# Narrow Fourier matmuls merged or left out, folded weights made in 64-column halves, rows of a coming pair loaded ahead of weight stores

## The chip, the cores and the metric
The kernel runs on one core of a Trainium2 chip. The metric is the device time of one execution in microseconds (us); several executions are timed and the median counts. One further execution was recorded by the profiler. A core has five engines that run side by side, each through its own instructions in order: TensorE (PE; its weight loads are listed as PEld), VectorE (DVE), ScalarE (ACT), GpSimd (POOL) and SyncE (SP), which here does nothing but issue transfers.

## The reference
Two sequences of 1024 tokens by 1024 features go through one encoder layer. Cut to what matters:

```python
mod = silu(c) @ w_ada + b_ada                      # shift, scale, gate, twice
h = rmsnorm(x, g_mix) * (1 + sc1) + sh1
z = h @ w_in                                       # q_lat 256 | kv_lat 128 | k_pe 64 | f_in 512
y_mla = mla_group(q_lat, kv_lat, k_pe, ...)        # 4 heads of attention from the latents
fr = real(fft2(f_in as (1024, 8 groups, 64), axes=(1, 3), norm='ortho'))
y_four = einsum('bsgc,gcd->bsgd', fr, w_four)      # 64 x 64 per group
x = x + ga1 * (concat([y_mla, y_four]) @ w_out)
h2 = rmsnorm(x, g_ffn) * (1 + sc2) + sh2
x = x + ga2 * ((silu(h2 @ w_gate) * (h2 @ w_up)) @ w_down)
return rmsnorm(x, g_final)
```

## The kernel before
All is float32. A large product is made exact enough by splitting both operands into a rounded high part and a remainder (`split`: a cast by ScalarE, a subtraction by VectorE, lines 60 and 61) and by three matmuls (`mm3`, lines 71 to 73). So most rows of TensorE read L71, L72 or L73, and the tile names tell them apart. Small products (L207, L303, L306, L744) are plain float32, and each of those leaves two records in the trace.

**Stage 1**, up to about 245 us. The tokens are taken in eight `pairs` (s, j): sequence s, and the rows of block j in both halves of the sequence (u = 0, 1). For a pair, `norm` loads its two row blocks `xt` (SP) and scales them (VectorE), `flip` transposes and modulates them, `zproj` makes the latents (`lat`, from the pool tag `sk` of three buffers), `latents` transposes and stores those, `evenodd` makes the sum and the difference of the two halves (`eoh`, `eol`), and `fourier_in` multiplies these by the input weights with the first cosine or sine transform folded in (`wcs_h`, `wcs_l`). Sums go to `zc`, differences to `zs`. For j = 0 another product gives the cosine columns of the difference's first row: `zo`, made of two token columns (24 matmuls, `128*2 128x280`). The cosine part holds 256 columns and 24 more, the Nyquist column of each of the eight groups three times over, for high part, high part and remainder.

`pair(k)` writes out this order, with the pieces of the generator `extras` between: at each `next(more)` it goes on to its next `yield`. Its last part folds the Fourier weights: `w4` (made into `lw`) times the last four chunks of `w_out` (`wo4`), times the gate `ga` of each sequence, stored to `wm_d` and `wn_d` (Nyquist rows). The products `so` take buffers of `sk` too.

**Stage 2**, about 245 to 349 us. `zsplit` splits `zc`, `zs` and `zo`, `dft` multiplies by the tables of the transform along the tokens (`tb`) into `A` (cosine), `B` (sine) and `ny` (Nyquist), `prep_wm` loads and splits the folded weights into `wm` and `wn`, and `fourier_out` makes, for a block j and a column half g, `pa` from A, wm and the 24-row product of `ny` and `wn` (L702), `pb` from B, and their difference and sum `ed`, which go to `fo_d`. For j = 0 the row of frequency 0 is put right: `dc_prep` makes `dl`, a product with it and two with columns of `ny` (L714, L715) go to three banks `pn`, and VectorE adds them to one row of `ed`. `mod2` (L744) makes the second modulation between. All accumulators come from eight banks.

**Stage 3**, from 349 us, is attention by blocks of 256 queries, and from about 1000 us to the end the FFN runs. Neither is changed. The loads for attention stand on SP between stores of `fo_d`.

Of the kernel before, what the change touches and what calls it, by code (L numbers as in the profile page):

```python
# [12 lines left out]
F32 = mybir.dt.float32  # L13
# [8 lines left out]
P = 128  # L22
# [22 lines left out]
NCS = NZC + NZS  # L45
NTE = 258
# [4 lines left out]
def hybrid_encoder_kernel(ctx: ExitStack, tc: tile.TileContext, a: dict):  # L51
# [33 lines left out]
    cmask = const.tile([P, 4], F32, name="cmask")  # L85
# [28 lines left out]
    wn_d = [dram.tile([NNYQ, D], F32, name=f"wn_d{s}") for s in range(2)]  # L114
# [39 lines left out]
    zo = [zp.tile([2, NZC], F32, name=f"zo{s}") for s in range(2)]  # L154

    with ExitStack() as st:
# [23 lines left out]
        lw = w.tile([P, 4, 2 * 64 + NNYQ], F32, name="lw")  # L180
# [72 lines left out]
        def small_weights():  # L253
            w4 = w.tile([P, 4, 2, GD], F32, tag="gah0", name="w4")
            nc.sync.dma_start(w4, a["w4"])
            for b in range(2):
                pr = slice(64 * b, 64 * b + 64)
                for k, op in enumerate((ALU.add, ALU.subtract)):
                    nc.vector.tensor_tensor(out=lw[pr, :, 64 * k + 32 * b : 64 * k + 32 * b + 32], in0=w4[pr, :, 0, 0:32],
                                            in1=w4[pr, :, 1, 0:32], op=op)  # L260
                for p in range(4):
                    o = P + 2 * p + b
                    nc.vector.tensor_copy(lw[pr, p, o : o + 17 : 8],
                                          w4[pr, p, 0, 32:33].broadcast_to([64, 3]))

        def extras():
# [27 lines left out]
            for g in range(2):  # L294
                gs = slice(512 * g, 512 * g + 512)
                ga = [w.tile([P, 512], F32, tag=f"gah{s}", name="gah") for s in range(2)]
                for s in range(2):
                    nc.sync.dma_start(ga[s], ga_d[32 * g + s, :].partition_broadcast(P))
                yield
                for p in range(5):  # L300
                    ps = bank()
                    if p < 4:
                        nc.tensor.matmul(ps, lw[:, p, :P], wo4[p // 2][:, p % 2, gs], start=True, stop=True)  # L303
                    else:
                        for q in range(4):
                            nc.tensor.matmul(ps[:NNYQ, :], lw[:, q, P:], wo4[q // 2][:, q % 2, gs], start=(q == 0), stop=(q == 3))  # L306
                    n = P if p < 4 else NNYQ
                    for s in range(2):
                        so = stile("so")
                        nc.vector.tensor_tensor(out=so[:n], in0=ps[:n], in1=ga[s][:n], op=ALU.mult)  # L310
                        if p < 4:
                            for k in range(2):
                                nc.sync.dma_start(wm_d[s][64 * (p % 2) : 64 * (p % 2) + 64, 2 * k + p // 2, gs],
                                                  so[64 * k : 64 * k + 64, :])
                        else:
                            nc.sync.dma_start(wn_d[s][:, gs], so[:n])
                    if p % 2 == 1:
                        yield
# [28 lines left out]

        def norm(k):
            s, j = pairs[k]
            ms = tiny.tile([P, 2], F32, name="ms")  # L350
            xt = []
            for u in range(2):
                t = xtile()
                nc.sync.dma_start(t, xs[s][rows(j, u), :])
                jk = w.tile([P, D], BF16, tag="junk", name="junk", bufs=1)
                nc.scalar.activation(jk, t, AF.Square, scale=1.0 / 32.0, accum_out=ms[:, u : u + 1])
                xt.append(t)
            r = rstd(ms, 2)
            for u in range(2):
                nc.vector.tensor_scalar(out=xt[u], in0=xt[u], scalar1=r[:, u : u + 1], scalar2=None, op0=ALU.mult)  # L360
            st1["x", k] = xt
# [76 lines left out]
        def fourier_in(k, i):  # L438
# [68 lines left out]
        def pair(k):  # L507
# [90 lines left out]
    with ExitStack() as st:  # L598
# [8 lines left out]
        zh, wms = {}, {}  # L607

        def zsplit(s):
            z = [[wa.tile([P, 4, n], F32R, tag=f"z{k}{i}", name=f"zh{k}{i}", bufs=1) for i in range(2)]  # L610
                 for k, n in enumerate((NZC, NZS))]
            od = [wa.tile([P, NZC], F32R, tag=f"zo{i}", name=f"zod{i}", bufs=1) for i in range(2)]
            for k, src in enumerate((zc[s], zs[s])):
                for c in range(0, 4, 2):
                    split(z[k][0][:, c : c + 2], z[k][1][:, c : c + 2], src[:, c : c + 2])
            for i in range(2):
                nc.vector.tensor_copy(od[i], rd(z[0][i][:, 0, :]))
            split(od[0][0:1, :], od[1][0:1, :], zo[s][0:1, :])
            zh[s] = (z, od)

        def dft(s):
# [3 lines left out]
            ny = w.tile([NNYQ, NT], F32R, tag="ny", name="ny", bufs=1)  # L625
            for q in (0, 2, 1):
                m = NNYQ if q == 2 else P
                sl = slice(P * q, P * q + m)
                pe, po = bank2(), bank2()
                for c in range(4):  # L630
                    mm3(pe[:m, :NTE], z[0][0][:, c, sl], z[0][1][:, c, sl], tb[0][0][:, c, :NTE], tb[0][1][:, c, :NTE],
                        c == 0, c == 3)
                for c in range(4):
                    zz = [od[i][:, sl] if c == 0 else z[0][i][:, c, sl] for i in range(2)]
                    mm3(po[:m, :256], zz[0], zz[1], tb[0][0][:, c, NTE:NT], tb[0][1][:, c, NTE:NT], c == 0, c == 3)
                if q == 2:
                    ah = w.tile([NNYQ, NT], F32R, tag="nyh", name="nyh", bufs=1)
                    al = w.tile([NNYQ, NT], F32, tag="nyl", name="nyl", bufs=1)
# [4 lines left out]
                if q == 2:  # L643
                    nc.vector.tensor_scalar(out=al, in0=al, scalar1=cmask[:m, 1:2], scalar2=None, op0=ALU.mult)
                    nc.vector.scalar_tensor_tensor(out=ny, in0=rd(ah), scalar=cmask[:m, 0:1], in1=al,
# [7 lines left out]
            return A, B, ny  # L653

        def prep_wm(s):
            wm = [w.tile([P, 4, D], F32R, tag=f"wm{i}", name=f"wm{i}", bufs=1) for i in range(2)]
            wn = w.tile([NNYQ, D], F32R, tag="wn", name="wn", bufs=1)
            for c in range(4):
                for g in range(2):
# [3 lines left out]
                    split(wm[0][:, c, gs], wm[1][:, c, gs], raw)  # L663
            for g in range(2):
                gs = slice(512 * g, 512 * g + 512)
                wnr = w.tile([NNYQ, 512], F32, tag="wnr", name="wnr", bufs=1)
                wnh = w.tile([NNYQ, 512], F32R, tag="wnh", name="wnh", bufs=1)
                nc.sync.dma_start(wnr, wn_d[s][:, gs])
                nc.scalar.copy(wnh, wnr)
                nc.vector.tensor_tensor(out=wnr, in0=wnr, in1=rd(wnh), op=ALU.subtract)  # L670
                nc.vector.tensor_scalar(out=wnr, in0=wnr, scalar1=cmask[:NNYQ, 3:4], scalar2=None, op0=ALU.mult)
                nc.vector.scalar_tensor_tensor(out=wn[:, gs], in0=rd(wnh), scalar=cmask[:NNYQ, 2:3], in1=wnr,
                                               op0=ALU.mult, op1=ALU.add)
            wms[s] = (wm, wn)

        def dc_prep(s, ABn):
            A = ABn[0]
            dl = [w.tile([P, 2, 2], F32R, tag=f"dl{i}", name=f"dl{i}", bufs=1) for i in range(2)]
            cd = w.tile([P, 2], F32, tag="cd", name="cd", bufs=1)
            ce = w.tile([P, 2], F32, tag="ce", name="ce", bufs=1)  # L680
            sub(cd, rd(A[0][:, :, 512]), rd(A[0][:, :, 0]), nc.vector)
            sub(ce, rd(A[1][:, :, 512]), rd(A[1][:, :, 0]), nc.vector)
            add(cd, cd, ce, nc.vector)
            for e in range(2):
                nc.vector.tensor_copy(dl[0][:, :, e], cd)
                nc.vector.tensor_tensor(out=dl[1][:, :, e], in0=cd, in1=rd(dl[0][:, :, e]), op=ALU.subtract)
            dls[s] = dl

        dls = {}

        def fourier_out(s, ABn, j):
# [3 lines left out]
            if j == 0:  # L695
                dl = dls.pop(s)
            for g in range(2):
# [23 lines left out]
        zsplit(0)  # L721
        tb[1] = [wa.tile([P, 4, 512], F32R, name=f"tb1{i}") for i in range(2)]
# [30 lines left out]
        for s in range(2):  # L753
            for j in (1, 2, 3, 0):
                fourier_out(s, abn, j)
                if j == 1:
                    dc_prep(s, abn)
# [751 lines left out]
def _constants():  # L1509
# [24 lines left out]
    cmask = np.zeros((P, 4))  # L1534
# [4 lines left out]
    cmask[8:16, 3] = 1  # L1539
    r = {  # L1540
# [55 lines left out]
```

## Time and profile before

| | us |
|---|---|
| median of 3 runs | 2136.97 (2136.36 to 2138.33) |
| the profiled execution | 2136.0 |
| its span | 2134.2 |
| mean granted clock of TensorE | 0.989 |

The profile covers the span; the 1.8 us between span and time lie around it, and the profiled execution is 0.97 us under the median. In a row of the timeline stand the start, the duration, engine, line, operation, out<-in, for a matmul the weights (rows by columns) and the streamed operand, the number of instructions that the row sums, and in brackets the engine's idle time before and what ended it. Matmuls overlap: the time that one costs is the distance from its start to the next start. In a row of the windows stand the window, its length, busy time and instructions of TensorE, of its weight loads, of VectorE, ScalarE and GpSimd, the granted clock, the DMA engines' busy share and GB/s.

### The profile page before, as it was taken

To read this page: it belongs to the slowest core of one execution; us is meant where nothing else is said; L and a number is where in the kernel's file an instruction comes from. 1 tells how busy PE (TensorE), PEld (TensorE's weight loads), DVE (VectorE), ACT (ScalarE), POOL (GpSimd) and SP (SyncE) were. 2 spreads that over 40 slices of the span, in tenths; PEclk is the share of its full clock that TensorE was granted. 3 is DMA by queue.
4 is the path that set the end of the run, shared out by engine and by line. 5 is a ranking of instruction groups with operands and counts; after the bars stand their busy time and mean duration, and the time that the engine had idled before them with its cause. 6 is when DMAs were issued, how large, how long until landed. Compare 5 with 4: busy or idle time off the path is not lost. (4 is left out here: it accounts for less than half of the span.)

```text
span 2134.2 us, 28930 instructions
## 1 busy us (share of the span) xinstructions
PE 2054.9 (96%) x10096; PEld 1671.4 (78%) x10096; DVE 1420.7 (67%) x2118; ACT 904.3 (42%) x1758; POOL 826.7 (39%) x1014
## 2 busy tenths in 40 slices
PE   5899998999999998999999999999999999999998
PEld 3787865888888886888888888887788888888876
DVE  2656655766676668786677667777866566557675
ACT  2655522555564546333333336444333333336441
POOL 1455202111222313797797720135545445420142
PEclk8999999999999999999999999999999999999999
DMA  9586656433545355564455468675423222248662
GB/s 366 189 248 181 225 189 234 102 92 92 138 119 124 119 182 203 187 212 168 159 206 188 153 227 290 226 237 175 148 79 119 99 101 97 99 135 290 230 226 101
DMA packets 184387, 371.11 MB, mean 174 GB/s; under 512 B 19280, under 2 KB 58832, under 8 KB 181168
## 3 DMA queue, kind: packets, MB, share of 16 engines
q1 hardware_dynamic: 166384, 313.80, 44.3%
q0 software_dynamic: 17856, 55.45, 8.8%
q8 instruction: 79, 1.29, 0.2%
q14 instruction: 68, 0.56, 0.1%
HBM read 257.18 MB, written 120.39 MB: 177 GB/s over the span
## 5 line engine op out<-in xcount | busy, mean ns | idle before, releaser
L71 PE MATMUL bank<-H,wh 128*128 128x512 f32 x1232 | 489.4, 397 | 13.5 <-DVE val L130 5.0
L73 PE MATMUL bank<-H,wl 128*128 128x512 f32 x1232 | 488.1, 396 | 1.5 <-DVE wl L61 1.5
L72 PE MATMUL bank<-H,wh 128*128 128x512 f32 x1232 | 488.2, 396 | 0.0
L130 DVE TENSOR_TENSOR val<-bank,val 128x512 f32<-128x512 f32 x244 | 167.0, 689 | 191.2 <-PE bank L73 183.4
L71 PEld LDWEIGHTS bank<-H,wh 128*128 128x128 f32 x1232 | 232.2, 188 | 73.2 <-DVE val L130 7.3
L73 PEld LDWEIGHTS bank<-H,wl 128*128 128x128 f32 x1232 | 232.0, 188 | 58.5 <-DVE wl L61 2.3
L72 PEld LDWEIGHTS bank<-H,wh 128*128 128x128 f32 x1232 | 232.0, 188 | 55.8
L61 DVE TENSOR_TENSOR wl<-draw,wh 128x512 fp32r<-128x512 f32 x286 | 200.9, 737 | 80.9 <-ACT wh L60 79.8
L60 ACT CAST wh<-draw 128x512 fp32r<-128x512 f32 x286 | 169.3, 619 | 155.3 <-PE bank L72 76.9
L72 PE MATMUL bank<-wl,wh 128*128 128x512 f32 x572 | 223.7, 391 | 2.2 <-DVE wl L61 2.2
L130 POOL TENSOR_TENSOR val<-val 128x512 f32<-128x512 f32 x58 | 82.8, 1434 | 363.5 <-DVE val L1380 188.6
L73 PE MATMUL bank<-wh,wl 128*128 128x512 f32 x572 | 222.6, 389 | 0.0
L71 PE MATMUL bank<-wh 128*128 128x512 f32 x572 | 222.6, 389 | 0.0
L60 ACT CAST wh<-rgu 128x512 fp32r<-128x512 f32 x172 | 106.7, 621 | 269.4 <-PE bank L72 211.5
L60 ACT CAST wh<-val 128x512 fp32r<-128x512 f32 x133 | 82.2, 621 | 277.6 <-PE bank L72 249.4
L61 DVE TENSOR_TENSOR wl<-val,wh 128x512 fp32r<-128x512 f32 x133 | 139.3, 1049 | 83.5 <-ACT wh L60 83.5
L61 DVE TENSOR_TENSOR wl<-rgu,wh 128x512 fp32r<-128x512 f32 x172 | 167.1, 972 | 4.8 <-ACT wh L60 4.2
L127 POOL TENSOR_TENSOR val<-rgu 128x512 f32<-128x512 f32 x84 | 122.0, 1452 | 120.3 <-DMA rgu<-in_wgu_dram 92.5
L72 PEld LDWEIGHTS bank<-wl,wh 128*128 128x128 f32 x572 | 107.3, 188 | 27.7 <-DVE wl L61 5.7
L71 PEld LDWEIGHTS bank<-wh 128*128 128x128 f32 x572 | 107.4, 188 | 22.3
L73 PEld LDWEIGHTS bank<-wh,wl 128*128 128x128 f32 x572 | 107.4, 188 | 22.1
L127 POOL TENSOR_TENSOR val<-val 128x512 f32<-128x512 f32 x89 | 119.4, 1358 | 1.3
(319 smaller groups left out, 4096.7 us busy)
## 6 DMA issues: line engine op xcount, KB each, us to landing
rgu<-in_wgu_dram SPq DMA_DIRECT2D x86, 512.0 KB, 4.2
draw<-s_d SPq DMA_DIRECT2D x143, 256.0 KB, 4.1
s_d<-val POOLq DMA_DIRECT2D x88, 256.0 KB, 4.1
draw<-t_d SPq DMA_DIRECT2D x88, 256.0 KB, 4.3
s_d<-val SPq DMA_DIRECT2D x66, 256.0 KB, 2.7
draw<-in_w_down_dram SPq DMA_DIRECT2D x55, 256.0 KB, 4.0
wada<-in_w_ada_dram SPq DMA_DIRECT2D x13, 1024.0 KB, 8.8
xt<-in_x_dram SPq DMA_DIRECT2D x16, 512.0 KB, 6.3
```

Source lines behind the costliest of these rows:

```text
L60: here["a"] = nc.scalar.copy(hi, src).ins
L61: here["v"] = nc.vector.tensor_tensor(out=lo, in0=src, in1=rd(hi), op=ALU.subtract).ins
L71: nc.tensor.matmul(out, lh, rh, start=first, stop=False, skip_group_check=cont)
L72: nc.tensor.matmul(out, lh, rl, start=False, stop=False, skip_group_check=cont)
L73: nc.tensor.matmul(out, ll, rh, start=False, stop=last, skip_group_check=cont)
L127: eng.tensor_tensor(out=out, in0=x, in1=y, op=ALU.subtract)
L130: eng.tensor_tensor(out=out, in0=x, in1=y, op=ALU.add)
```

## The change
1. `zo` of both sequences is made at once, at pair (1, 0): four token columns `zoc`, two of each sequence, which VectorE copies aside; the row of sequence 1 is moved to a tile of its own by a transfer.
2. The fold is made by chunk c of `wm`: the two 64-column halves of `lw` that make a chunk go to partitions 0 to 63 and 64 to 127 of one bank, one store of 128 rows takes the place of two of 64, and the Nyquist rows are no product of their own: they are rows 0, 32, 64 and 96 of the sine chunks, stored three times over by a transfer (`wn_d`), and put to zero in `wm` by a column of `cmask`, when `wm` is split.
3. The Nyquist columns of both sequences are split together (`nyq_split`) and go through `dft` once, 48 columns wide, at sequence 0. `ny` and `wn` are padded with zero rows to 128; `cmask` picks the sequence's rows.
4. `dc_prep` goes. The DC row is made by columns 512 and 513 of A and `ny` in one bank, and ScalarE copies it over the row of `ed`.
5. `x_load(k + 2)`, the loads of `norm(k + 2)`, stands before the third `next(more)` of pair k, and no longer after it.

```diff
-    zo = [zp.tile([2, NZC], F32, name=f"zo{s}") for s in range(2)]
+    zo = [zp.tile([ZOW, NZC], F32, name="zo"), zp.tile([1, NZC], F32, name="zo1")]
...
-                for p in range(5):
+                for c in range(4):
+                    k, i = c // 2, c % 2
                     ps = bank()
-                    if p < 4:
-                        nc.tensor.matmul(ps, lw[:, p, :P], wo4[p // 2][:, p % 2, gs], start=True, stop=True)
-                    else:
-                        for q in range(4):
-                            nc.tensor.matmul(ps[:NNYQ, :], lw[:, q, P:], wo4[q // 2][:, q % 2, gs], start=(q == 0), stop=(q == 3))
+                    for q in range(2):
+                        nc.tensor.matmul(ps[64 * q : 64 * q + 64, :], lw[:, 2 * i + q, 64 * k : 64 * k + 64], wo4[i][:, q, gs],
+                                         start=True, stop=True)
                     for s in range(2):
                         so = stile("so")
...
+                        nc.vector.tensor_tensor(out=so, in0=ps, in1=ga[s], op=ALU.mult)
+                        nc.sync.dma_start(wm_d[s][:, c, gs], so)
+                        if k == 1:
+                            nc.sync.dma_start(
+                                wn_d[NNYQ * s : NNYQ * s + NNYQ, gs].rearrange("(k r) n -> r k n", k=3)[4 * i : 4 * i + 4],
+                                so[0:97:32, :].unsqueeze(1).broadcast_to([4, 3, 512]))
...
             if i == 1 and j == 0:
+                for k in range(2):
+                    nc.vector.tensor_copy(zoc[k][:, :, 2 * s : 2 * s + 2], rd(eo[1][k][:, :, 0:2]))
+            if i == 1 and j == 0 and s == 1:
                 po = bank()
                 for c in range(NC):
-                    mm3(po[:2, :NZC], eo[1][0][:, c, 0:2], eo[1][1][:, c, 0:2], wcs_h[:, c, :NZC], wcs_l[:, c, :NZC],
+                    mm3(po[:ZOW, :NZC], zoc[0][:, c, :], zoc[1][:, c, :], wcs_h[:, c, :NZC], wcs_l[:, c, :NZC],
                         c == 0, c == NC - 1)
-                nc.vector.tensor_copy(zo[s], po[:2, :NZC])
+                nc.vector.tensor_copy(zo[0], po[:ZOW, :NZC])
+                nc.sync.dma_start(zo[1], zo[0][2:3, :])
...
+            if k + 2 < nk:
+                x_load(k + 2)
             next(more, None)
...
+        nyt = w.tile([P, NT], F32R, name="ny")
+        nc.vector.tensor_scalar(out=nyt, in0=raws[0, 0], scalar1=0.0, scalar2=None, op0=ALU.mult)
...
-            for q in (0, 2, 1):
-                m = NNYQ if q == 2 else P
+            for q in (0, 2, 1) if s == 0 else (0, 1):
+                m = NY2 if q == 2 else P
...
-                wnr = w.tile([NNYQ, 512], F32, tag="wnr", name="wnr", bufs=1)
-                wnh = w.tile([NNYQ, 512], F32R, tag="wnh", name="wnh", bufs=1)
-                nc.sync.dma_start(wnr, wn_d[s][:, gs])
+                wnr = w.tile([P, 512], F32, tag="wnr", name="wnr", bufs=1)
+                wnh = w.tile([P, 512], F32R, tag="wnh", name="wnh", bufs=1)
+                nc.gpsimd.memset(wnr, 0.0)
+                nc.sync.dma_start(wnr[:NY2], wn_d[:, gs])
...
                 if j == 0:
-                    pn = [bank2() for _ in range(3)]
+                    pn = bank2()
                     for q in range(2):
-                        mm3(pn[0][:2, :], dl[0][:, q, :], dl[1][:, q, :], wm[0][:, q, gs], wm[1][:, q, gs], q == 0, q == 1)
-                    nc.tensor.matmul(pn[1][:2, :], ny[:, 512:514], wn[:, gs], start=True, stop=True)
-                    nc.tensor.matmul(pn[2][:2, :], ny[:, 0:2], wn[:, gs], start=True, stop=True)
-                    for q, f in enumerate((add, add, sub)):
-                        f(ed[1][0:1, :], ed[1][0:1, :], pn[q][0:1, :], nc.vector)
+                        mm3(pn[:2, :], A[0][:, q, 512:514], A[1][:, q, 512:514], wm[0][:, q, gs], wm[1][:, q, gs], q == 0, False)
+                    nc.tensor.matmul(pn[:2, :], ny[:, 512:514], wn[:, gs], start=False, stop=True)
+                    nc.scalar.copy(ed[1][0:1, :], pn[0:1, :])
```

Where the instructions stand, in the rows' own words (the line, the operation, out<-in, the shape of the output and the count; lines 71 to 73 before are 73 to 75 after). TensorE at the first fold burst, before, where `ident,xt` is a flip and `wcs_h,eoh` is `fourier_in`:

```order
L431 MATMUL bank<-ident,lat 128x128 x4
L374 MATMUL bank<-ident,xt 128x128 x8
L303 MATMUL bank<-wada,lw 128x512 x2
L71 MATMUL bank<-wcs_h,eoh 128x280
L72 MATMUL bank<-wcs_l,eoh 128x280
```
and at the first of the two 24-column bursts, where `wz_h,hh` is `zproj`:

```order
L73 MATMUL bank<-wz_h,hl 128x448
L374 MATMUL bank<-ident,xt 128x128 x8
L306 MATMUL bank<-wada,lw 24x512 x4
L71 MATMUL bank<-wz_h,hh 128x448
L72 MATMUL bank<-wz_l,hh 128x448
```
After, at the first fold burst:

```order
L432 MATMUL bank<-ident,lat 128x128 x4
L375 MATMUL bank<-ident,xt 128x128 x8
L304 MATMUL bank<-wada,lw 64x512 x4
L73 MATMUL bank<-wcs_h,eoh 128x280
L74 MATMUL bank<-wcs_l,eoh 128x280
```
Four products of 64 columns stand where two of 128 stood, and no burst stands between the flip and `zproj` any more.

TensorE at the end of a unit for j = 0, from the last product of B on, before:

```order
L73 MATMUL bank<-wm_3394,B_3262 128x512
L71 MATMUL bank<-wm_3394,dl_3544 2x512
L72 MATMUL bank<-wm_3395,dl_3544 2x512
L73 MATMUL bank<-wm_3394,dl_3545 2x512
L71 MATMUL bank<-wm_3394,dl_3544 2x512
L72 MATMUL bank<-wm_3395,dl_3544 2x512
L73 MATMUL bank<-wm_3394,dl_3545 2x512
L714 MATMUL bank<-wn,ny 2x512
L715 MATMUL bank<-wn,ny 2x512
L71 MATMUL bank<-wm_3394,A_3259 128x512
L72 MATMUL bank<-wm_3395,A_3259 128x512
L73 MATMUL bank<-wm_3394,A_3260 128x512
```
After:

```order
L75 MATMUL bank<-wm_3305,B_3210 128x512
L73 MATMUL bank<-wm_3305,A_3207 2x512
L74 MATMUL bank<-wm_3306,A_3207 2x512
L75 MATMUL bank<-wm_3305,A_3208 2x512
L73 MATMUL bank<-wm_3305,A_3207 2x512
L74 MATMUL bank<-wm_3306,A_3207 2x512
L75 MATMUL bank<-wm_3305,A_3208 2x512
L726 MATMUL bank<-wn,ny 2x512
L73 MATMUL bank<-wm_3305,A_3207 128x512
L74 MATMUL bank<-wm_3306,A_3207 128x512
L75 MATMUL bank<-wm_3305,A_3208 128x512
```
Of eight two-column matmuls seven are left, all into one bank.

SP around the fold's first stores, before (`lat_d` and `ckv_d` are latents that are stored):

```order
L354 DMA xt<-in_x_dram 128x1024
L422 DMA ckv_d_98<-kv 128x128
L422 DMA ckv_d_99<-kv 128x128
L313 DMA wm_d_86<-so 64x512 x2
L313 DMA wm_d_87<-so 64x512 x2
L313 DMA wm_d_86<-so 64x512 x2
L313 DMA wm_d_87<-so 64x512 x2
L436 DMA lat_d_94<-lh 512x1x128
L436 DMA lat_d_95<-ll 512x1x128
```
After:

```order
L349 DMA xt<-in_x_dram 128x1024
L423 DMA ckv_d_97<-kv 128x128
L423 DMA ckv_d_98<-kv 128x128
L309 DMA wm_d_86<-so 128x512
L309 DMA wm_d_87<-so 128x512
L349 DMA xt<-in_x_dram 128x1024
L309 DMA wm_d_86<-so 128x512
L309 DMA wm_d_87<-so 128x512
L437 DMA lat_d_93<-lh 512x1x128
L437 DMA lat_d_94<-ll 512x1x128
L309 DMA wm_d_86<-so 128x512
L311 DMA wn_d<-so 4x3x512
```
The second row block of the coming pair is loaded after two stores of 128 rows; before, sixteen of 64 rows and two transfers of latents are ahead of it (its own row comes after those shown). A store of the small `wn_d` follows each store of a sine chunk.

More of the change, by code (lines that the diff above doesn't have):

```diff
@@ L45 @@
 NCS = NZC + NZS
+NY2 = 2 * NNYQ
+ZOW = 4
 NTE = 258
@@ L113, in hybrid_encoder_kernel @@
     wm_d = [dram.tile([P, 4, D], F32, name=f"wm_d{s}") for s in range(2)]
-    wn_d = [dram.tile([NNYQ, D], F32, name=f"wn_d{s}") for s in range(2)]
+    wn_d = dram.tile([NY2, D], F32, name="wn_d")
     hc_d = [dram.tile([P, 4, 4, 512], F32, name=f"hc_d{s}") for s in range(2)]
@@ L179, in hybrid_encoder_kernel @@
         c2 = w.tile([P, P], F32, name="c2")
-        lw = w.tile([P, 4, 2 * 64 + NNYQ], F32, name="lw")
+        lw = w.tile([P, 4, P], F32, name="lw")
+        zoc = [w.tile([P, NC, ZOW], F32R, name=f"zoc{i}") for i in range(2)]
         cT = w.tile([P, NC, 2], F32, name="cT")
@@ L260, in small_weights @@
                                             in1=w4[pr, :, 1, 0:32], op=op)
[L261 to L264, printed above, removed]
+                nc.vector.tensor_copy(lw[pr, :, 64 + 32 * b], w4[pr, :, 0, 32])
         def extras():
@@ L346, in hybrid_encoder_kernel, with x_load @@
         st1 = {}
+        def x_load(k):
+            s, j = pairs[k]
+            st1["x", k] = [xtile() for _ in range(2)]
+            for u in range(2):
+                nc.sync.dma_start(st1["x", k][u], xs[s][rows(j, u), :])
         def norm(k):
-            s, j = pairs[k]
+            if ("x", k) not in st1:
+                x_load(k)
             ms = tiny.tile([P, 2], F32, name="ms")
-            xt = []
+            xt = st1["x", k]
             for u in range(2):
-                t = xtile()
-                nc.sync.dma_start(t, xs[s][rows(j, u), :])
+                t = xt[u]
                 jk = w.tile([P, D], BF16, tag="junk", name="junk", bufs=1)
                 nc.scalar.activation(jk, t, AF.Square, scale=1.0 / 32.0, accum_out=ms[:, u : u + 1])
-                xt.append(t)
             r = rstd(ms, 2)
@@ L662, in prep_wm @@
                     nc.sync.dma_start(raw, wm_d[s][:, c, gs])
-                    split(wm[0][:, c, gs], wm[1][:, c, gs], raw)
+                    if c < 2:
+                        split(wm[0][:, c, gs], wm[1][:, c, gs], raw)
+                    else:
+                        nc.scalar.activation(wm[0][:, c, gs], raw, AF.Copy, scale=cmask[:, 6:7])
+                        nc.vector.scalar_tensor_tensor(out=wm[1][:, c, gs], in0=raw, scalar=cmask[:, 6:7],
+                                                       in1=rd(wm[0][:, c, gs]), op0=ALU.mult, op1=ALU.subtract)
@@ L669, in prep_wm @@
                 nc.scalar.copy(wnh, wnr)
                 nc.vector.tensor_tensor(out=wnr, in0=wnr, in1=rd(wnh), op=ALU.subtract)
-                nc.vector.tensor_scalar(out=wnr, in0=wnr, scalar1=cmask[:NNYQ, 3:4], scalar2=None, op0=ALU.mult)
-                nc.vector.scalar_tensor_tensor(out=wn[:, gs], in0=rd(wnh), scalar=cmask[:NNYQ, 2:3], in1=wnr,
+                nc.vector.tensor_scalar(out=wnr, in0=wnr, scalar1=cmask[:, 3 + 2 * s : 4 + 2 * s], scalar2=None, op0=ALU.mult)
+                nc.vector.scalar_tensor_tensor(out=wn[:, gs], in0=rd(wnh), scalar=cmask[:, 2 + 2 * s : 3 + 2 * s], in1=wnr,
@@ L721, in hybrid_encoder_kernel @@
         zsplit(0)
+        nyq_split()
         tb[1] = [wa.tile([P, 4, 512], F32R, name=f"tb1{i}") for i in range(2)]
@@ L1539, in _constants @@
     cmask[8:16, 3] = 1
+    cmask[24:48, 0:2] = cmask[0:24, 0:2]
+    cmask[24:48, 4:6] = cmask[0:24, 2:4]
+    cmask[:, 6] = np.arange(P) % 32 != 0
     r = {
```

75 lines of the change are left out of this document (31 added, 44 removed).

## The prediction
> **What bounds the kernel now.** I read the page's list of engines first, then the chain that ended last, then the stretches of the first 400 us, in which every edit lies, and there the timeline of each engine.
>
> ```profile
> PE 2054.9 (96%) x10096; PEld 1671.4 (78%) x10096; DVE 1420.7 (67%) x2118; ACT 904.3 (42%) x1758; POOL 826.7 (39%) x1014
> ...
> PE 26%; DMA 1%; DVE 0%; POOL 0%; ACT 0%; issue 0%; SPq 0%; DVEq 0%; POOLq 0%; ACTq 0%
> ```
> ```profile
> 100.00:200.00 100.00, 100.00 (x626) 81.91 (x625) 59.34 (x121) 61.73 (x153) 52.99 (x114) 1.00 0.75 221
> 200.00:300.00 100.00, 95.50 (x522) 70.58 (x521) 62.06 (x127) 41.67 (x99) 18.73 (x44) 1.00 0.74 238
> 300.00:350.00 50.00, 48.71 (x241) 33.88 (x241) 32.30 (x75) 15.18 (x33) 0.00 (x0) 1.00 0.55 193
> 350.00:400.00 50.00, 41.92 (x235) 35.01 (x234) 37.23 (x72) 25.90 (x49) 16.68 (x14) 0.90 0.38 126
> ```
> The first number after the comma is TensorE's busy time, the last but two its granted clock. TensorE is busy for 100.00 of 100 us in the fold's stretch, 95.50 and 48.71 of 50 in the Fourier stage, at full clock; only from 350 on does it wait (41.92 of 50, clock 0.90). So a matmul that goes before 350 us is worth its start-to-start time, unless an engine behind it was already late. That is the method below: start of the next other matmul minus start of the first.
>
> **Nyquist row of the odd half (`zo`), 48 matmuls to 24.**
> ```profile
> 174.98 0.29 PE L71 MATMUL bank<-wcs_h,eoh 128*2 128x280 f32 x1
> 178.09 0.36 PE L71 MATMUL bank<-wz_h,hh 128*128 128x448 f32 x1
> ```
> ```profile
> 87.94 3.47 DVE L360 TENSOR_SCALAR xt<-xt,rs_r 128x1024 f32<-128x1024 f32 x2 [2.01 <-POOL rs_r L102]
> ```
> ```profile
> 93.29 0.93 PE L374 MATMUL bank<-ident,xt 128*128 128x128 f32 x7
> ```
> 24 of them last 178.09 − 174.98 = 3.11 us. The set that goes is sequence 0's, in pair 0. It was also cover: the flip of pair 2 starts at 93.29 and would be wanted at 90.2, but its rows are scaled by VectorE until 87.94 + 3.47 = 91.41, behind a GpSimd result that the edit doesn't hurry. I take a wait of 1.2 (bounds 0, if the earlier `x_load` hurries the squares, and 1.2): −1.9.
>
> **Folded Fourier weights in halves.** Before: four bursts of two 128-column products and two bursts of four 24-column ones. After: four bursts of four 64-column products, which write to the two halves of one bank.
> ```profile
> 165.17 1.88 PE L303 MATMUL bank<-wada,lw 128*128 128x512 f32 x4
> ...
> 167.01 0.29 PE L72 MATMUL bank<-wcs_l,eoh 128*128 128x280 f32 x1
> 167.14 0.29 PE L73 MATMUL bank<-wcs_h,eol 128*128 128x280 f32 x1
> ...
> 183.86 3.61 PE L306 MATMUL bank<-wada,lw 128*24 128x512 f32 x8
> ...
> 187.72 0.37 PE L72 MATMUL bank<-wz_l,hh 128*128 128x448 f32 x1
> 187.92 0.37 PE L73 MATMUL bank<-wz_h,hl 128*128 128x448 f32 x1
> ```
> ```profile
> 268.49 0.39 PE L73 MATMUL bank<-wm,B 128*128 128x512 f32 x1
> 268.81 1.92 PE L744 MATMUL bank<-wada,scT 128*32 128x512 f32 x16
> ...
> 271.00 0.39 PE L72 MATMUL bank<-wm,A 128*128 128x512 f32 x1
> 271.23 0.40 PE L73 MATMUL bank<-wm,A 128*128 128x512 f32 x1
> ```
> A plain fp32 product leaves two records. Take off the one matmul that stands between burst and second row (0.13, 0.20): 167.01 − 165.17 − 0.13 = 1.71, so 0.43 a record, and 187.72 − 183.86 − 0.20 = 3.66. Entering a narrow burst costs another 268.81 − 268.49 − 0.23 = 0.09. Before: 4 × 1.71 + 2 × (3.66 + 0.09) = 14.3. The nearest row to the new form is L744: 16 records of 32 columns, four column groups side by side, in 271.00 − 268.81 − 0.23 = 1.96, that is four rounds of 0.43 and 0.25 for leaving. Two groups of 64 columns side by side need four rounds for eight records as well: 4 × (1.96 + 0.09) = 8.2. That is −6.1. The other bound is no overlap, 32 × 0.43 + 4 × 0.34 = 15.1, or +0.8. I take −6.1, since L744 differs only in the width of the group.
>
> ```profile
> L71 PEld LDWEIGHTS bank<-H,wh 128*128 128x128 f32 x1232 | 232.2, 188 | 73.2 <-DVE val L130 7.3
> ```
> Against this speaks the Trainium skill, TensorEngine Tiling (Array Packing), Tile-to-Partition Mapping, under its restrictions: column tiling switches the fast weight load off. Were each of the 32 loads then exposed for half of the 0.188 of the row above, an estimate, the saving would be −3.1 instead. The L744 row shows sixteen records with their loads in 1.96, so nothing is exposed there, and the sum goes by it.
>
> SP issues 32 + 4 stores of these weights before, 16 + 8 after; what they store is read only in the next stage. `x_load` moves the rows of a coming pair ahead of some of them on SP. TensorE was busy 100.00 of 100 us there, so there is no wait that an earlier load could heal: 0.
>
> **DFT of the Nyquist columns, once for both sequences.**
> ```profile
> 304.94 0.28 PE L71 MATMUL bank<-tb,zh 128*24 128x258 f32 x1
> ...
> 307.75 0.28 PE L71 MATMUL bank<-tb,zh 128*128 128x258 f32 x1
> ```
> The second set of 24 goes: −2.81. The set left has 48 columns instead of 24 and keeps its time, since the rows streamed set it: 2 columns by 280 take 3.11 / 24 = 0.13 each, and 128 columns by 280 the same 0.13 (167.01 to 167.14). The new splits (`nyq_split`, six VectorE steps of 96 columns or less) come after those that the first product waits for and before the sine tables, which TensorE reaches three groups of 2.8 later: 0.
>
> **The DC column and the `ny`·`wn` product.**
> ```profile
> 340.57 0.39 PE L71 MATMUL bank<-wm,dl 128*2 128x512 f32 x1
> ...
> 342.91 0.39 PE L72 MATMUL bank<-wm,A 128*128 128x512 f32 x1
> ...
> 343.84 0.40 PE L73 MATMUL bank<-wm,A 128*128 128x512 f32 x1
> 344.17 0.50 PE L702 MATMUL bank<-wn,ny 24*128 24x512 f32 x1
> 344.59 0.50 PE L71 MATMUL bank<-wm,B 128*128 128x512 f32 x1
> 344.93 0.39 PE L72 MATMUL bank<-wm,B 128*128 128x512 f32 x1
> ```
> Eight matmuls took 342.91 − 340.57 − 0.23 = 2.11; seven of 0.233 take 1.63: −0.48, four times −1.9. Around the 24-row product the starts lie 0.33, 0.42 and 0.34 apart, where 128-row ones lie 0.233 apart: 0.39 too much, in 16 places. The edit pads both operands to 128 rows, so the form is that of its neighbours: 16 × −0.39 = −6.2 (the other bound is 0, if something else makes the steps). VectorE also drops twelve one-row sums.
>
> The padding adds a GpSimd memset ahead of the load of `wnr`, in a single buffer:
> ```profile
> 0.90 0.60 POOL L462 MEMSET lw<- 128x608 f32 x1
> ```
> ```profile
> 265.01 0.31 SPq L668 DMA_DIRECT2D wnr<-wn_d  x1
> ```
> ```profile
> 269.93 0.74 DVE L672 SCALAR_TENSOR_TENSOR wn<-wnh,cmask,wnr 24x512 fp32r<-24x512 f32 x1
> ```
> ```profile
> 271.56 0.50 PE L702 MATMUL bank<-wn,ny 24*128 24x512 f32 x1
> ```
> The second load waits for the first chain, then for 0.60 of memset and a hop; behind it on SP stand a load of `wm` and the stores. The product at 271.56 has 0.9 us to spare after 270.67. I take +0.5 (0 to 1) in sequence 0; in sequence 1 the loads are long done.
>
> **The end of the Fourier stage.** In sequence 1 TensorE saves 2.8 + 8 × 0.39 + 0.96 = 6.9. VectorE is late there:
> ```profile
> 341.19 0.69 DVE L127 TENSOR_TENSOR ed<-ea,bank 128x512 f32<-128x512 f32 x1 [6.63 <-DMA fo_d<-ed]
> ```
> ```profile
> 331.36 16.03 SPq L719 DMA_DIRECT2D fo_d<-ed  x12
> ```
> ```profile
> 349.47 0.39 PE L71 MATMUL gb<-wq_h,ql 128*128 128x256 f32 x1 [1.29 <-DVE ed L130]
> ```
> It stands 6.63 us until a store of `fo_d` lands behind the attention stage's loads, while TensorE fills the eight banks. Those loads start after the first unit, so the landing moves by 2.8 + 0.4 only, to 338.0. Four units are then left, of two 0.69 steps each: 338.0 + 5.5 = 343.5, while TensorE itself is done at 349.47 − 1.29 − 6.9 = 341.3. The next stage starts near 343.6 instead of 349.47: −5.9 of the 6.9. Sequence 0 gives 8 × −0.39 − 0.96 + 0.5 = −3.6.
>
> **The first steps of attention**, unchanged in code:
> ```profile
> 364.59 0.36 PE L71 MATMUL gb<-ql,wq_h 128*128 128x256 f32 x1 [2.77 <-DVE qt L855]
> ...
> 374.84 1.71 PE L915 MATMUL ppt<-ident,p 128*128 128x128 f32 x8 [2.03 <-DVE pt L61]
> ```
> ```profile
> 364.00:380.00 16.00, 12.33 (x45) 9.66 (x46) 10.23 (x20) 8.50 (x17) 6.96 (x5) 0.68 0.31 106
> ```
> The 2.77 and 2.03 are VectorE's backlog, and the low clock costs up to 16 × 0.32 = 5.1. VectorE comes in without the six one-row sums of sequence 1 behind it; against that, TensorE comes 1 us earlier to it. Bounds −6 and +2; I take −2, since most of this chain is its own.
>
> **Sum.** `zo` −1.9, fold −6.1, Fourier stage −3.6 and −5.9 (the −2.8 is in the second), attention −2: −19.5. The profiled execution took 2136.0, 2134.2 of it the span, and lies 0.97 under the median; the difference is taken from the median: 2136.97 − 19.5 = 2117.5.
>
> **Rivals.**
> A. The column halves run one after the other: +0.8 in place of −6.1, 2124.4. For: no 64-column row in the trace. Against: L744. 8%.
> B. Padding to 128 rows doesn't take the 0.39 away, because changing to the small `wn` operand makes it: 2123.7. Against: L71 changes operands from A to B without a step. 8%. The Trainium skill, TensorEngine Tiling (Array Packing), Key Properties, says that a change of tiling mode drains the array; a product of 24 rows among ones of 128 would then pay on entering and on leaving, as the 0.33 and 0.34 show, and B would be out.
> C. The landing of `fo_d` ends the stage wholly: the transfers before it are set by the DMA queues and come no earlier within sequence 1, so the 3.2 by which I moved the landing go: 2121. For: SP's row, 16.03 us for twelve stores, most of it waiting. Against: the loads ahead of it are issued by VectorE's and ScalarE's steps, which follow TensorE. 18%.
> D. Attention's entry heals: gaps halved and the clock full, −8 in place of −2: 2111.5. 11%. The Trainium skill, TensorE: Matmul & The Clock Gate, part 1, ties the half clock to an idle window of about 3.4 us; here the clock is low after gaps of 2.77 at most, so the trace is stricter than the page, and a small change of the gaps may switch it either way.
> E. Slower: eight extra small stores read `so` from the pool `sk`, three buffers that `lat` and `modrow` share. If SP's order holds those buffers, the latents' product waits:
> ```profile
> PE bank L431 <- DVE lat L416: 1.8, 2, 1.6
> ```
> It decides once the eight cost TensorE over 2.5 us each (8 × 2.5 = 20), so 2140. Against: SP issues no more stores in all, and the wait listed is 1.8 in all between 100 and 250. 3%.
>
> **Numbers.** The likeliest (52%, 2114 to 2121) gives 2117.5. With A, B and C the range ends at 2126, with D at 2109; outside lie E, A with B together, and a full healing. A difference of 0.2% (4.3 us) is about what can be told from none here: faster 0.94, within 0.03, slower 0.03.
>
> **What would show it.** Right: the four fold bursts take about 2.0 each; starts around the `ny` product are 0.23 apart; one set of 48-column products; attention's first product at 332 (349.47 − 17.5). Wrong: fold bursts of 3.4 (A), steps of 0.33 left (B), a longer TensorE gap on `ed` (C), a clock of 1.00 where 0.68 stood (D), waits of L431 (E).

## The result, and the profile after

The changed kernel takes 2119.58 us in the median of five runs (2115.77 to 2122.14) against 2136.97 before: a ratio of 0.9908, with a 95% interval of 0.9897 to 0.9920, or 17.4 us less. The forecast was 2117.5. A later series of the same kernel gave 2117.94 against 2138.75, ratio 0.9903 (0.9890 to 0.9917). The profiled execution shown here took 2122.14, 2120.3 of it the span: 13.9 less than the profiled execution before.

The page after, the engines, and from the windows the stretches shown before (columns as there):

```profile
PE 2038.2 (96%) x10044; PEld 1671.6 (79%) x10044; DVE 1405.4 (66%) x2087; ACT 906.1 (43%) x1763; POOL 825.1 (39%) x1018
```
```profile
100.00:200.00 100.00, 100.00 (x650) 82.33 (x649) 62.06 (x128) 62.38 (x152) 54.83 (x120) 1.00 0.73 231
200.00:300.00 100.00, 95.79 (x565) 78.22 (x563) 65.27 (x132) 48.58 (x116) 17.94 (x42) 0.98 0.69 232
300.00:350.00 50.00, 41.63 (x197) 32.37 (x195) 26.57 (x60) 16.92 (x33) 8.11 (x8) 0.97 0.71 246
350.00:400.00 50.00, 48.88 (x305) 43.12 (x306) 40.65 (x76) 28.31 (x55) 10.77 (x11) 0.96 0.39 101
```
TensorE's busy time fell by 16.7 us (2054.9 to 2038.2), and in the fold's stretch it is still 100.00 of 100: what was taken out there was on the path.

From TensorE's timeline, a fold burst and what follows it:

```profile
163.65 1.94 PE L304 MATMUL bank<-wada,lw 128*64 128x512 f32 x8
165.52 0.40 PE L73 MATMUL bank<-wcs_h,eoh 128*128 128x280 f32 x1
165.75 0.29 PE L74 MATMUL bank<-wcs_l,eoh 128*128 128x280 f32 x1
165.88 0.29 PE L75 MATMUL bank<-wcs_h,eol 128*128 128x280 f32 x1
```
165.75 − 163.65 − 0.13 = 1.97 for eight records. And the unit for j = 0:

```profile
282.54 0.40 PE L73 MATMUL bank<-wm,A 128*2 128x512 f32 x1
...
284.17 0.40 PE L73 MATMUL bank<-wm,A 128*128 128x512 f32 x1
...
285.33 0.39 PE L75 MATMUL bank<-wm,A 128*128 128x512 f32 x1
285.56 0.40 PE L714 MATMUL bank<-wn,ny 128*128 128x512 f32 x1
285.79 0.40 PE L73 MATMUL bank<-wm,B 128*128 128x512 f32 x1
```
Seven two-column matmuls take 284.17 − 282.54 = 1.63, and the starts around the padded product lie 0.23 apart.

From the timelines of VectorE, SP and TensorE, the end of the Fourier stage and the first steps of attention:

```profile
326.26 0.69 DVE L129 TENSOR_TENSOR ed<-ea,bank 128x512 f32<-128x512 f32 x1 [5.61 <-DMA fo_d<-ed]
```
```profile
316.81 15.64 SPq L729 DMA_DIRECT2D fo_d<-ed  x14
```
```profile
331.50 0.39 PE L73 MATMUL gb<-wq_h,ql 128*128 128x256 f32 x1 [1.47 <-DVE ed L132]
...
347.85 0.55 PE L73 MATMUL gb<-ql,wq_h 128*128 128x256 f32 x1 [5.90 <-DVE qt L864]
```
Attention starts at 331.50 in place of 349.47. The same instructions of the two traces, put side by side, give the lead of the changed kernel on its way:

| place in the program (time before) | lead, us |
|---|---|
| first flip of pair 2 (93.4) | 1.3 |
| before the first fold burst (143.7) | 1.6 |
| after the last one (213.4) | 8.0 |
| sequence 0's last `mod2` (300.1) | 11.2 |
| sequence 1's last DFT group (307.8) | 14.0 |
| first attention product (349.5) | 18.0 |
| attention's second block (447.5) | 20.5 |
| 690.6 | 19.6 |
| 758.9 | 17.7 |
| 859.2 to 875.6 | 17.5 to 16.2 |
| 1557.2 | 14.9 |
| end | 13.9 |

The lead grows until 447 about as the steps of the forecast add up, and then 6.6 us are lost in code that the change does not touch. That loss is what the first experiments ask about. One more loss hides in the table: from 231.06 to 234.47 us this profile ran at half clock (0.50), behind a wait of 1.96 us for `lat` (1.60 before), and the lead fell from 8.3 to 6.7 there, 1.3 of it in that step, before it grew on. The second profile below has no such step; its lead goes from 7.1 to 11.4 between the last fold burst and sequence 0's last `mod2`.

### The profile page after: what moved, and what is told of

Same layout as the page of the kernel before. It is cut to its first block, busy times and chain, and to the rows that moved or that the text cites. A ratio compares the mean times of both kernels' runs of the same rounds, so it can differ in the third digit from the quotient of the medians.

```text
span 2120.3 us, 28781 instructions
## 1 busy us (share of the span) xinstructions
PE 2038.2 (96%) x10044; PEld 1671.6 (79%) x10044; DVE 1405.4 (66%) x2087; ACT 906.1 (43%) x1763; POOL 825.1 (39%) x1018
```

## The experiments

Each edit is made to the changed kernel and each kernel is timed against the kernel before.

**The changed kernel again.** No edit.

> The changed kernel, nothing edited, a second look. In its first profile the lead over the kernel before was 20.5 us at 450 us into the program and 13.9 at the end, all lost in code that the change does not touch. Theory G (grid): the clock of TensorE is granted in steps of 3.41 us that are not tied to the program's start; a step in which TensorE stood still for more than about 1.9 us is followed by one at half clock. So the same short waits cost 0 or 0.9 to 1.7 us by where the steps fall. Then this profile shows half-clock steps at partly other places between 400 us and the end (seven there in the first: at 668, 726, 811 twice, 1467, 1514), and the runs lie between 2114 and 2123 with a lower mean clock for the longer ones. Rival W (new waits): the moved transfers made waits of their own in attention and FFN; then the lead is lost at the same places again (690, 760, 835, 1530), by the same 0.9, 1.6, 1.5 and 1.3 us, and the runs do not follow the clock.

Measured: 2117.94 us (2116.97 to 2120.50); the profiled execution took 2116.97. The windows of one clock step each, around the two stops of 2.07 us in attention that both kernels have. Of the kernel before:

```profile
682.51:685.92 3.41, 2.39 (x17) 1.75 (x16) 2.22 (x2) 2.54 (x7) 3.08 (x7) 1.00 0.27 77
685.92:689.34 3.42, 2.37 (x12) 2.02 (x12) 3.31 (x7) 1.21 (x2) 3.18 (x3) 1.00 0.84 197
```
of the changed kernel, first profile:

```profile
664.56:667.97 3.41, 1.46 (x6) 1.24 (x7) 3.31 (x7) 1.24 (x3) 3.33 (x3) 1.00 0.41 106
667.97:671.39 3.42, 3.42 (x16) 3.19 (x14) 2.41 (x2) 0.57 (x1) 1.43 (x2) 0.50 0.78 208
722.59:726.00 3.41, 1.34 (x7) 0.89 (x8) 3.41 (x5) 1.45 (x4) 3.41 (x3) 1.00 0.29 61
726.00:729.41 3.41, 3.41 (x10) 2.67 (x9) 2.46 (x5) 0.94 (x2) 2.46 (x3) 0.50 0.84 221
```
and of the same kernel, second profile:

```profile
665.79:669.20 3.41, 1.94 (x8) 1.61 (x9) 3.30 (x7) 1.21 (x2) 3.33 (x3) 1.00 0.72 169
669.20:672.61 3.41, 3.07 (x27) 2.90 (x26) 3.11 (x5) 1.38 (x3) 0.96 (x2) 1.00 0.76 170
```
The last number but two is the granted clock. Before, a step's edge cut the stop in two halves (2.39 and 2.37 busy of 3.41), and the clock stayed at 1.00. In the first profile the whole stop fell into one step (1.46 busy), and the next ran at 0.50; in the second the edge cut it again (1.94 busy in the step that held the larger part), and it stayed at 1.00. So the same wait in the same kernel cost half clock once and nothing once. Half-clock steps between 400 us and 1600: two before, six in the first profile, three in the second. Four more steps at half clock can cost 4 × 3.41 / 2 = 6.8; paired instruction by instruction, 5.3 of the 6.6 lie in such steps and 1.0 in longer waits. In the second profile 1.9 lie in half-clock steps and shorter waits win 1.9 back: the lead is 19.1 at 450 and 19.0 at the end. Theory G explains most of the loss. W keeps a small part: the wait before one product of the FFN is longer in both profiles of the changed kernel. Before (a wait of 0.14, which the row doesn't list), then in the first profile (1.15 in the second):

```profile
875.59 0.50 PE L71 MATMUL bank<-H,wh 128*128 128x512 f32 x1
```
```profile
859.42 0.50 PE L73 MATMUL bank<-H,wh 128*128 128x512 f32 x1 [1.52 <-ACT val L1288]
```
What makes it longer no run shows. Another mark was missed: the runs don't follow the clock's mean, 0.984 to 0.988 with 2120.50 at 0.984 but 2116.97 and 2117.97 both at 0.988; the first 93 us, in which TensorE waits for loads, differ by up to 2.5 us between the profiles.

**Longer waits.** In `norm2`, the second line added:

```diff
         nc.vector.tensor_scalar(out=xn, in0=x2, scalar1=r[:, 0:1], scalar2=None, op0=ALU.mult)
+        nc.vector.tensor_scalar(out=xn, in0=x2, scalar1=r[:, 0:1], scalar2=None, op0=ALU.mult)
```

> The changed kernel, but VectorE scales each block of normed rows (xn) twice over, the same values again, 1.75 us more ahead of the row maximum. Theory G (clock steps of 3.41 us on a grid of their own; half clock follows a step with more than about 1.9 us of standstill): the two waits of 2.07 us become about 3.8, which no place of the grid can split into less than 1.9, so each is followed by half clock in every execution; the waits of 1.08 become about 2.8 and are followed by half clock in about three of four cases. Then 4 x 1.75 to 6 x 1.75 = 7 to 10.5 of waiting and 0.9 to 1.7 for each of five half steps: 12 to 18 us more than the changed kernel, and half steps at about 440, 500, 560, 670 and 730 where its profiles show none or two. Rival: half clock has nothing to do with the length of the wait; then only the 7 to 10.5 are added and the number of half steps between 400 and 800 stays at 0 to 2.

Measured: 2123.95 us (2119.43 to 2126.55), 4 to 6 us more than the changed kernel, less than expected. The stops grew by 1.1 and not by 1.75 (3.20 and 3.21 us), and only one of the three small ones grew (2.04). The windows at the two long ones:

```profile
663.59:667.00 3.41, 0.26 (x3) 0.06 (x1) 3.41 (x6) 0.31 (x1) 3.33 (x3) 1.00 0.08 21
667.00:670.42 3.42, 3.37 (x8) 2.70 (x9) 2.01 (x4) 0.90 (x2) 1.86 (x2) 0.50 0.49 119
725.02:728.44 3.42, 1.22 (x5) 1.05 (x6) 3.41 (x6) 1.21 (x2) 3.04 (x3) 1.00 0.00 0
728.44:731.85 3.41, 3.41 (x14) 3.05 (x14) 2.26 (x3) 0.33 (x1) 0.41 (x1) 0.50 0.81 193
```
Both are followed by half clock, as G has it. But these two are the only half-clock steps between 400 and 800 us, where five were expected; the rival allowed up to two, and the first profile of the changed kernel has two as well. So this run fits G without deciding for it. What decides is the count over all profiles, in the last section.

**Only 48 rows streamed.** The padding undone in the products:

```diff
-                nc.tensor.matmul(pa, ny[:, js], wn[:, gs], start=False, stop=True)
+                nc.tensor.matmul(pa, ny[:NY2, js], wn[:NY2, gs], start=False, stop=True)
```
(and the same in the two-column product)

> The changed kernel, but the products of ny and wn stream only their 48 filled rows in place of 128 (all 16 of them and the four two-column ones); the result is the same. Theory: the extra 0.39 us of each was made by the narrow contraction, and padding took it away. Then the steps around each are 0.33, 0.42 and 0.34 again (0.23 now), 16 x 0.39 = 6.2 us more at the start of attention, of which sequence 1's half may partly hide behind VectorE (stage 2 longer by 4 to 6.5). Rival B: the small operands themselves made it and another part of the change removed it; then the steps stay at 0.23 and attention starts within 0.5 us of 331.5.

Measured: 2125.66 us (2123.58 to 2127.78), 7.7 more than the changed kernel beside it. TensorE's timeline:

```profile
288.49 0.40 PE L75 MATMUL bank<-wm,A 128*128 128x512 f32 x1
288.82 0.49 PE L714 MATMUL bank<-wn,ny 48*128 48x512 f32 x1
289.24 0.50 PE L73 MATMUL bank<-wm,B 128*128 128x512 f32 x1
289.57 0.39 PE L74 MATMUL bank<-wm,B 128*128 128x512 f32 x1
```
The steps are 0.33, 0.42 and 0.33 again. Counted from 235 us (this profile has a half-clock step at 231), and against the changed kernel's second profile, TensorE's last Fourier matmul comes 7.1 later (the two-column products pay too), but attention starts only 4.5 later, since the wait for VectorE before it (2.51 there) is gone: some 2.5 us of what padding saves had turned into that wait. Rival B falls.

**Fold products in another order.** The two products of a burst's first half come first, then the two of the second:

```diff
-                    for q in range(2):
-                        nc.tensor.matmul(ps[64 * q : 64 * q + 64, :], ...)
+                    for q in range(2):
+                        for c in cs:
+                            nc.tensor.matmul(pss[c][64 * q : 64 * q + 64, :], ...)
```

> The changed kernel, but of the four 64-column products of a fold burst the two of the first half of the bank come first and then the two of the second (the same products, two banks open). If halves run side by side only when neighbours in the queue go to different halves, a burst takes three lengths of a product in place of two: 3 x 0.86 = 2.6 us in place of 1.7 between entry and exit, 0.85 more in each of four bursts, and the forecast's 6.1 shrinks to 2.7. Rival: TensorE looks further ahead and the bursts stay at 1.94.

Measured, in one run: 2117.88 us, and the burst

```profile
163.12 1.94 PE L306 MATMUL bank<-wada,lw 128*64 128x512 f32 x8
```
It stays at 1.94. Products for different column halves ran side by side though two of the same half stood in a row in the program. In the trace the second product of the burst starts 0.014 us behind the first, and 0.006 in the changed kernel, as if one product were passed over. The rival holds, and the forecast's row (L744) was a safe one to go by.

**Loads not ahead.** The two lines with `x_load(k + 2)` taken out of `pair`.

> The changed kernel without the early x_load: the rows of a coming pair are loaded where norm asks for them, behind the stores of the folded weights. Prediction: worth 0, because TensorE never waits in the fold's stretch; TensorE's busy time from 100 to 200 us stays 100 of 100 and the time within 1 us of the changed kernel. Rival: loads behind the 24 stores come late enough for the flip; then TensorE waits for xt between 165 and 215 us, 1 to 4 us.

Measured: 2118.32 us (2117.49 to 2119.93), as the changed kernel (2117.94 and 2119.58). TensorE's busy time from 100 to 200 us:

```profile
100.00:200.00 100.00, 100.00 (x650) 82.59 (x643) 62.22 (x126) 62.22 (x153) 54.83 (x120) 1.00 0.74 232
```
Worth 0, as forecast.

**GpSimd issues sequence 1's stores.**

```diff
-                    nc.sync.dma_start(fo_d[s][rows(j, u), gs], ed[u])
+                    (nc.gpsimd if s == 1 else nc.sync).dma_start(fo_d[s][rows(j, u), gs], ed[u])
```

> The changed kernel, but sequence 1's stores of fo_d are issued by GpSimd, which is idle there, and not by SP, where they stand behind attention's loads. VectorE stands 5.61 us until 326.26 in the changed kernel for a landing of them, and TensorE 1.5 to 2.5 us at the end of the stage for VectorE. If SP's order makes that (SP stands 3.3 us at 311.2 for a buffer with six finished stores behind it): VectorE's stop falls under 2 us, TensorE's wait for ed goes, attention starts 1.5 to 2.5 us earlier. Rival C (the transfers themselves are the bound): the stop stays near 5 us and attention starts within 0.7 us of before.

Measured: 2116.32 us (2113.97 to 2118.36). VectorE's waits, by what released them, of the changed kernel and then of this one:

```profile
DVE ed L129 <- DMA fo_d<-ed: 5.6, 1, 5.6
```
```profile
DVE wv L63 <- ACT wv L62: 4.6, 1, 4.6
...
DVE ed L129 <- DMA fo_d<-ed: 1.3, 1, 1.3
```
Attention starts at 327.47, without a wait for `ed`: the finished stores had stood on SP behind loads that waited for a buffer. That is not rival C, the transfers themselves. Not all of the 4.0 us to 331.50 is the edit's: this profile is 2.4 ahead at 300 us already, by its start and by the half-clock step at 231 that the first profile has and this one has not. Counted from there, attention starts 1.7 sooner than in the first profile and 2.7 sooner than in the second, about the 1.5 to 2.5 expected. The time is 1 to 3 us less than the changed kernel's, which is not clear of the noise; the next wait (`wv`) has grown from 3.3 to 4.6 us.

**The first `wv` splits behind the maximum.**

```diff
-            split(wv[0][:, h, gs], wv[1][:, h, gs], S.pop(("wv", h, g)))
+            with tc.issue_after(here["nb"]), tc.issue_after(here["ex"]):
+                split(wv[0][:, h, gs], wv[1][:, h, gs], S.pop(("wv", h, g)))
```

> The changed kernel, with the splits of the gated output weights (wv) queued on VectorE and ScalarE behind the row maximum and the exponential of the scores that stand before them in the program. In the changed kernel VectorE stands 3.33 us at 343.03 for the first of them, ahead of the maximum's scaling, and TensorE stands 5.90 us until 347.85, with half clock for 6.83 us after it. If that order makes the wait: TensorE's stop shrinks to 1 to 2 us, the half clock there goes, time 4 to 7 us less than the changed kernel (about 2113). Rival: TensorE waits there for VectorE's other work (rotation, maxima) or for loads that come late anyway; then the stop stays over 4 us and the time within 2 us of the changed kernel's 2118 to 2120.

Measured: 2118.08 us (2113.70 to 2118.47), no gain. But the stop of 5.90 is 0.83:

```profile
342.98 0.50 PE L898 MATMUL ps_s<-lat,qa 128*128 128x512 f32 x1 [0.83 <-ACT qa L62]
```
and from 300 us to 447 its profile wins 6.4 us on the second one of the changed kernel. Between 560 and 670 us, where sequence 1's `wv` is split, 3.5 of these go again, 2.0 of it new stops of TensorE, and a half-clock step stands at 663. The edit was right in one place and wrong in the other. The profiled execution, 2113.70, is the fastest of the four; why the other three take 2118 no trace shows.

**`xn` behind the maximum.** The scaling of `xn` in `issue_after(here["nb"])`.

> The changed kernel, with the scaling of the normed rows (xn, VectorE, 1.75 us) queued behind the scaled maximum of the scores before it. Two waits of TensorE of 2.07 us each (664.44 and 723.62 in the changed kernel's profile, released by the maximum) stand behind that step in both kernels. Theory G says that they cost 2.07 each, and 0.9 and 1.6 more where a clock step holds the whole of one. Expected: both waits under 1 us, none followed by half clock, 2 to 5 us less than the changed kernel, and a narrower spread of the runs. Rival: the wait moves to the next user of VectorE (the flips of the scaled scores), then waits of 1.5 to 2 us appear a few us later and the time stays within 1 us.

Measured: 2115.92 us (2114.31 to 2121.85), the stops still 2.07 and 2.09. VectorE's timeline:

```profile
661.46 1.74 DVE L819 TENSOR_SCALAR xn<-x,rs_r 128x1024 f32<-128x1024 f32 x1 [3.69 <-ACT ht L832]
663.13 1.21 DVE L908 TENSOR_REDUCE mx<-ps_s 128x1 f32<-128x1024 f32 x1
```
`xn` was put behind the maximum of the step before and stayed ahead of the one that TensorE waits for. The edit missed its target; its question is answered below.

**`xn` by ScalarE**, with the `wv` edit for the first sequence alone:

```diff
-        nc.vector.tensor_scalar(out=xn, in0=x2, scalar1=r[:, 0:1], scalar2=None, op0=ALU.mult)
+        nc.scalar.activation(xn, x2, AF.Copy, scale=r[:, 0:1])
```

> The changed kernel with two edits in attention: the first sequence's wv splits (not the second's, which cost 2.2 us of new waits around 600 to 630 when they were queued so too) behind the maximum and the exponential, and xn scaled by ScalarE in place of VectorE. If the stops of 5.90 and 2 x 2.07 were VectorE's order, they shrink to under 1 us each, and the half clock after them goes: 7 us at the entry as in the earlier run, 2 to 4 at the two stops, so 2108 to 2112. Rival: ScalarE's step comes late in its own queue and delays the exponentials; then new waits on p or nb of 1 to 2 us stand at the same places and the time is 2112 to 2116.

Measured: 2124.11 us (2121.21 to 2125.13), 4.5 to 6.2 more than the changed kernel. TensorE's waits from 400 to 800 us:

```profile
PE ppt L924 <- ACT qp L877: 8.4, 6, 1.4
PE ppt L924 <- ACT ht L831: 6.8, 6, 1.2
```
15 us of waits for ScalarE stand where 7.4 for the maximum stood. The rival holds, and its price was set too low. No step between 320 and 800 us ran at half clock, since no stop came near 1.9: the clock did what G says, the waits alone cost the time.

**Both edits at the entry**, the `wv` order for the first sequence alone:

> The changed kernel with two edits at the entry of attention: sequence 1's fo_d stores issued by GpSimd (alone: attention started at 327.5 in place of 331.5, and ScalarE's and VectorE's wait for the first wv split was then 4.6 us, with TensorE's stop of 3.75 behind it), and the first sequence's wv splits queued behind the maximum and the exponential (alone: the stop of 5.90 became 0.83). If the two are separate waits, they add up: attention starts near 327.5, no stop over 1.3 us follows in its first 20 us and no half clock, 8 to 10 us less than the changed kernel at 450 us into the program, 2108 to 2113 in all. Rival: one wait hides the other, then the lead at 450 us is 4 to 7 us and the time 2112 to 2116.

Measured: 2110.71 us (2108.55 to 2113.73), 6 to 9 less than the changed kernel, as expected. But the traces don't show two separate waits that add up. The same stretch, from the last Fourier unit to attention's second block, takes 99.9 and 101.5 us in the two profiles of the changed kernel, 94.8 with the stores edit alone, 95.1 with the `wv` edit alone and 93.2 with both. TensorE stands in it for 9.5 and 11.2 us, then for 6.0, 5.5 and 4.2, and has two and three half-clock steps, then one in each. So either edit alone wins most of what both win there. A stop of 2.66 at 347 for ScalarE's exponential is left, with one half-clock step after it, which the expectation excluded. So the right time came in part for another reason than the one given.

**And `xn` a step later**, its scaling traced in the next step of the loop, behind that step's scaled maximum:

```diff
+        if i in (2, 4):
+            S.pop("scale")()
```

> As fo_wv, and xn is scaled by VectorE one step of the loop later, behind that step's scaled maximum (the earlier try put it behind the maximum of the step before, which left the order as it was). If VectorE's wait for GpSimd's rs_r and the 1.75 of xn ahead of the maximum make the stops of 2.07 and 1.08 in attention, those shrink to under 0.6, 2 x 1.5 + 3 x 0.6 = about 5 us less than fo_wv, and half clock is not seen between 400 and 790: 2104 to 2109. Rival: xn comes later for the flips of the normed rows; then stops of 1 us or more stand at pht<-ident,xn and the time is that of fo_wv or more.

Measured: 2103.56 us (2102.86 to 2105.06), ratio to the kernel before 0.9841 (0.9827 to 0.9854). TensorE's waits in attention, without this edit and with it:

```profile
PE ps_s L900 <- DVE nb L908: 7.4, 5, 2.1
```
```profile
PE ps_s L909 <- DVE qa L63: 1.0, 2, 0.5
```
The five stops are gone, no step from 330 to 780 us runs at half clock (two follow at 781.5, where the expectation had none up to 790), and the five runs lie within 2.2 us, where those of the changed kernel spread over 6.4 and 3.5. This is the fastest version here: 13 to 16 us less than the changed kernel.

## Why the prediction was right, point by point

- **`zo`, −1.9.** The 24 matmuls went; the flip's wait for `xt` came as named, 0.79 us in the first profile:

```profile
92.12 0.66 PE L375 MATMUL bank<-ident,xt 128*128 128x128 f32 x4 [0.79 <-DVE xt L362]
```
and 0.81 + 1.34 in the second. So the term is −2.3 or −1.0; the bound of 1.2 for the wait was too tight by 1.
- **Fold, −6.1.** Bursts of 1.97 against a forecast 1.96. The lead grew by 6.4 from the first to the last burst. Rival A falls with that. The rule of the Trainium skill, TensorEngine Tiling (Array Packing), Tile-to-Partition Mapping, that column tiling switches the fast weight load off, cost nothing that shows: the loads of the halves are inside the 1.97, so the −3.1 estimated from it did not come.
- **DFT, −2.8.** The lead went from 11.2 to 14.0.
- **Sequence 0, −3.6.** The lead grew by 3.2 in the first profile, which lost 1.6 by the wait for `lat` and the half clock at 231 us, and by 4.3 in the second.
- **DC, −1.9, and `ny`·`wn`, −6.2.** 1.63 and 0.23, as forecast; the second shown by the run with 48 rows. That a product of narrow operands costs an entry and an exit (0.33, 0.34) agrees with the drain at a change of tiling mode of which the Trainium skill speaks, TensorEngine Tiling (Array Packing), Key Properties.
- **Memset, +0.5.** No wait shows; 0.
- **End of the stage.** VectorE was to go on at 338.0 less the 11.6 won before, 326.4; it did at 326.26. TensorE done at 330.03, attention at 331.50, forecast 332. The landing moved as the argument said, so rival C fell; the store order on SP was its cause.
- **Entry of attention, −2.** The lead grew by 2.5, and by 2.0 in the second profile, but not as described: the stop of 2.77 became 5.90 (6.57 in the second), those of 2.03 and four smaller ones nearly went, and the half-clock steps there are two and three against three before. The size was right by luck. D did not come: the half clock stayed.
- **What the sum lacked** is the unchanged rest, above all its clock: 6.6 us lost in the first profile (5.3 at half clock), 0.1 in the second. The sum, 19.5, holds at 447 us (20.5 and 19.1); the medians, 17.4 and, in the second series, 20.8, have more or less of the later loss. No step of the forecast speaks of it, so that the medians come this close to 2117.5 is partly luck. Rival D named the mechanism at one place only.
- **E** fell: TensorE has no wait for `lat` in the fold's stretch; the one behind it grew from 1.60 us (before) to 1.96 and 1.98, and in the first profile half clock followed it.

## What to carry to other kernels

On a path that TensorE sets, price a removed or merged matmul by the distance of starts, take an existing row of the same shape for a new one, and ask at each place what the removed work covered. Narrow products cost their full stream, and a contraction of few rows among full ones costs its change of form on both sides: pad it. A stop of TensorE of about 2 us can cost up to 1.7 us more (half of a clock step; 1.05 at 668 and at 726 in the first profile) by where it falls on the clock's grid, so after a gain look for such stops in the code that was not changed. Taking out five stops of 1.1 to 2.1 us won 7.1 us here (2110.71 to 2103.56), about as much as the largest part of the change, the padding (7.7 by the run without it). And time edits that meet at one stop together: each alone may win most of what both win.

## What the runs showed of the hardware

- The granted clock goes in steps of 3.41 us, on a grid that is not tied to the program's start: in the thirteen profiles its offset from there runs from 0.19 to 3.30 us. Counting steps at full clock from 60 us to TensorE's last matmul, every one of the 61 with 1.92 us or more of standstill of TensorE was followed by a step at half clock, and none with 1.70 or less; between, both occurred. The Trainium skill, TensorE: Matmul & The Clock Gate, part 1, says that the window is free-running, which the traces bear out, and gives an idle window of about 3.4 us as the condition; here a little over half of one was enough.
- Products for the two column halves of a bank ran side by side though two of the same half came first in the program: bursts of 1.94 in both orders (one run).
